# Stick-breaking attention summed by parts, and six of its gates computed as pairs of half-size products

## The chip, the cores and the metric

The kernel runs on one core of one Trainium2 chip, as one program. The metric is the device time of one execution in microseconds (us). Engines are named as in the profile: PE (TensorE matmul), DVE (VectorE), ACT (ScalarE), POOL (GpSimd), SP (SyncE, which here issues nearly all the DMAs from one queue).

## The reference, cut to what matters

One layer with two token mixers over 1024 tokens of width 1024, in float32. The normalized input h is multiplied by one wide matrix; its columns give, for a gated linear attention (GLA, 4 heads), queries, keys, values, gates and a decay code, for stick-breaking attention (8 heads of 128) queries, keys, values and gates, and two merge gates. Each branch is projected, gated and merged; an output projection and a norm follow. What the change touches is stick-breaking:

```
z = q . k / sqrt(d)                       # for every query t and key s
log1m = where(s < t, log_sigmoid(-z), 0)
between = reversed cumsum(log1m) - log1m  # sum over s < j < t
A = where(s < t, exp(log_sigmoid(z) + between), 0)
o = A @ v                                 # then o * silu(s_gate)
```

With beta = sigmoid(z), A[t,s] = beta[t,s] times the product of 1 - beta[t,j] over s < j < t. Let P[t,s] be the product of 1 - beta[t,j] over s <= j < t. Then A[t,s] = P[t,s+1] - P[t,s], and summation by parts turns the sum of A[t,s] v[s] into the sum of P[t,s] (v[s-1] - v[s]) plus one term of v.

## The kernel before, in words

Every float32 operand of a matmul is split into a high part (an ACT copy to float32r, line 165) and a low part (a DVE subtraction, line 166), and each product is three matmuls: high-high, high-low, low-high. Matmuls stream 512 columns where they can.

**Stages in order.** (1) The input is normed and transposed; the four quarters of h (token half by parity of the 128-wide block of D) are held as `a11`, `a12`, `a21`, `a22`. In the same stage a first group of 256 columns of a value projection is computed directly (`first_v`, with the decay code in the same matmuls), and three more groups follow (`v_unit`, `vjobs`): 24 matmuls of 256 columns for each of 8 token blocks. (2) Projections as **pairs** (`pair_job`, lines 235 to 301): two 128-wide column blocks at once in seven half-size products of 12 matmuls each (Strassen's scheme in Winograd's form), so 84 matmuls of 512 columns for 256 output columns and all tokens, against 96 for the direct way. A pair has seven *units*; `Pairs.run(n)` issues n units, with the loads and splits of the next pairs between them. The first 22 units run between the steps of the GLA decays, the units up to number `GLA_AT` between loads, sums and stores of later weights (`tjobs`); in both stretches the order on ACT and DVE is the order of the program. (3) GLA: 32 steps, each with four units of pairs (137 units in all from its start to its last step). (4) **Stick-breaking**, then (5) the merge and the output projection, again as half-size products.

**Stick-breaking** runs over 8 heads of 8 query blocks of 128. For block i, `scores` multiplies queries and keys of the causal prefix (banks `z`, two), takes sigmoid(-z) into `eb` and sigmoid(z) into `be` (ACT, lines 960 and 961), scans `eb` from the right on DVE (line 964, a running product with the diagonal block masked), masks `be` on POOL (line 965) and multiplies the two on DVE (line 968). Two steps later `turn` transposes the result block by block on PE (line 980) and splits it into `near` (diagonal half) and `far` buffers. `values` multiplies these with the split values: 12 matmuls for the first four blocks of a head, 24 for the last four, and multiplies the sum with the gate (line 1004). Queries are loaded two blocks at a time, four steps ahead; keys and values one head ahead.

**Filler.** Between the steps stand *units* of 24 matmuls (`proj_t`): the silu gates of the eight heads in two token halves (16 units) and the first projection of GLA's output (`pa`, 16 units). Two run ahead of the first head; `SB_PLAN` says how many run at each step: three per head (at steps 3 and 6 ahead of the transposes, at step 7 behind them). `line` lists the units in order, with their weight loads and with two loads of GLA's outputs (`o_dma`), which overwrite the quarters of h once the gates no longer read them. Six units are left for the start of stage 5.

**Who sets the order.** Outside the stretches with a manual schedule, the order of each engine's instructions is laid down at build time by a planner that simulates the program and prefers earlier program lines among what is ready; in the trace the matmuls of one filler unit therefore often stand in several places between those of the scores. At run time each engine takes its instructions in that order.

## Time and profile before

| | |
|---|---|
| time, median of 3 runs | 1204.47 us (1201.83 to 1204.98) |
| the profiled execution's own time, and its span | 1205.73 us, 1204.0 us |
| PE busy | 1185.2 us, 98% of the span, 6087 matmuls |
| DVE / ACT / POOL busy | 855.4 (71%) / 555.8 (46%) / 316.7 us (26%) |
| mean granted PE clock | 0.997 |
| moved by DMA | 247.67 MB, mean 206 GB/s |
| first value groups and sums | from the start to about 114 us |
| eight pairs ahead of GLA / GLA with pairs / stick-breaking | 116 to 276, 276 to 711, 720 to 1010 us |

In the profile, a group's row gives line, engine, operation, tiles and shapes, the count, then busy us and mean ns of one, then the engine's idle time just before and what ended it. Matmuls overlap in the pipeline: the mean duration of one is longer than the distance from one start to the next, so PE's work is read from stretches of time, not from durations. `PEld` are weight loads, which run beside the matmuls. A row of stretches gives busy time and number of instructions of each engine between two times.

### The profile page before, as it was taken

The page shows a single profiled execution, that of the slowest core. Times are in us where ns is not written, and L with a number is a line of the kernel's source. Part 1 is how long each engine was busy: PE and PEld are TensorE (multiplying, and loading weights), DVE is VectorE, ACT ScalarE, POOL GpSimd, SP SyncE. Part 2 cuts the span into 40 slices and gives each one's busy share as a digit, 9 for nine tenths or more (in the row PEclk, how much of TensorE's full clock was granted, in tenths as well). Part 3 has the DMA queues.
Part 4 walks back from the last instruction along what each step waited for, and adds up shares of the span by engine and source line. Part 5 has one row for each costly group of instructions (what it writes and reads, how often), then busy time and mean ns, then how long its engine had stood idle before and what let it go on. Part 6 is the DMA issues. An engine that isn't in the chain of part 4 may idle for free.

```text
span 1204.0 us, 17310 instructions
## 1 busy us (share of the span) xinstructions
PE 1185.2 (98%) x6087; PEld 997.8 (83%) x6087; DVE 855.4 (71%) x1341; ACT 555.8 (46%) x1081; POOL 316.7 (26%) x303
## 2 busy tenths in 40 slices
PE   8999999999999999999999999999999999999997
PEld 8999878888888888888888887888878888788886
DVE  5475876896676676776674646777787775578986
ACT  5343763334334444444443425445455553365543
POOL 1486513243322322422323201111021110700001
PEclk9999999999999999999999999999999999999999
DMA  7545349988546646666655267564788547758652
GB/s 282 182 140 154 136 164 337 338 303 265 185 145 197 179 157 210 209 200 204 218 172 166 80 230 259 168 209 159 251 263 304 169 131 242 254 161 282 225 192 105
DMA packets 207090, 247.67 MB, mean 206 GB/s; under 512 B 12662, under 2 KB 141708, under 8 KB 205468
## 3 DMA queue, kind: packets, MB, share of 16 engines
q1 hardware_dynamic: 206428, 245.52, 62.3%
q8 instruction: 48, 0.79, 0.3%
q10 hardware_dynamic: 576, 1.05, 0.2%
q14 instruction: 38, 0.31, 0.1%
HBM read 154.25 MB, written 92.27 MB: 205 GB/s over the span
## 4 chain that ended last, share of the span: by engine, by line
PE 83%; DVE 7%; DMA 3%; ACT 3%; issue 3%; SPq 1%; POOL 0%; DVEq 0%; ACTq 0%
PE pp L270 12%; PE pp L272 12%; PE pp L271 12%; PE pp L223 8%; PE pp L204 4%; PE pp L206 4%; PE pp L205 4%; PE av L1002 2%; PE av L1003 1%; PE z L956 1%; PE av L1001 1%; PE tr L980 1%; PE xb L1368 1%; PE xb L1367 1%; PE z L957 1%
## 5 line engine op out<-in xcount | busy, mean ns | idle before, releaser
L166 DVE TENSOR_TENSOR wl<-tt,wh 128x1024 fp32r<-128x1024 f32 x56 | 70.6, 1261 | 49.6 <-ACT wh L165 49.4
L965 POOL TENSOR_SCALAR_AFFINE_SELECT be<-be 128x128 f32<-128x128 f32 x64 | 38.0, 595 | 236.7 <-ACT be L961 218.3
L309 DVE TENSOR_TENSOR f<-pp,f 128x512 f32<-128x512 f32 x84 | 57.8, 688 | 59.1 <-PE pp L272 55.7
L964 DVE TENSOR_TENSOR_SCAN eb<-eb,m 128x128 f32<-128x128 f32 (+3 forms) x64 | 86.7, 1356 | 9.7 <-ACT eb L960 9.5
L165 ACT ACTIVATE wh<-tt 128x1024 fp32r<-128x1024 f32 x56 | 59.3, 1059 | 67.2 <-PE pp L271 63.8
L244 POOL TENSOR_TENSOR tt<-raw 128x512 f32<-128x512 f32 x28 | 39.5, 1412 | 190.9 <-DVE wl L166 184.2
L165 ACT ACTIVATE wh<-raw 128x1024 fp32r<-128x1024 f32 x47 | 49.7, 1059 | 81.0 <-PE pp L271 39.1
L276 ACT ACTIVATE f<-pp 128x512 f32<-128x512 f32 x84 | 49.7, 592 | 79.9 <-PE pp L272 79.9
L166 DVE TENSOR_TENSOR wl<-raw,wh 128x1024 fp32r<-128x1024 f32 x47 | 70.5, 1501 | 22.4 <-ACT wh L165 21.6
L231 POOL TENSOR_TENSOR r<-r,nhalf 128x1 f32<-128x1 f32 x40 | 24.2, 604 | 193.2 <-DVE r L230 182.7
L960 ACT ACTIVATE eb<-z 128x384 f32<-128x384 f32 (+4 forms) x96 | 48.8, 508 | 43.4 <-issue 22.8
L968 DVE TENSOR_TENSOR be<-be,eb 128x128 f32<-128x128 f32 (+3 forms) x64 | 48.3, 757 | 3.6
L961 ACT ACTIVATE be<-z 128x384 f32<-128x384 f32 (+4 forms) x96 | 49.2, 513 | 0.0
L270 PE MATMUL pp<-ha22h,wh 128*128 128x512 f32 x112 | 44.7, 399 | 0.3 <-DVE f L309 0.2
L270 PE MATMUL pp<-ha11h,wh 128*128 128x512 f32 x112 | 44.5, 397 | 0.0
L270 PE MATMUL pp<-ha12h,wh 128*128 128x512 f32 x112 | 44.5, 397 | 0.0
L270 PE MATMUL pp<-S1h,wh 128*128 128x512 f32 x112 | 44.4, 396 | 0.0
L270 PE MATMUL pp<-S3h,wh 128*128 128x512 f32 x112 | 44.1, 394 | 0.0
L270 PE MATMUL pp<-S2h,wh 128*128 128x512 f32 x112 | 44.0, 392 | 0.0
L270 PE MATMUL pp<-S4h,dh 128*128 128x512 f32 x112 | 43.9, 392 | 0.0
L271 PE MATMUL pp<-ha22l,wh 128*128 128x512 f32 x112 | 43.7, 390 | 0.0
L272 PE MATMUL pp<-ha22h,wl 128*128 128x512 f32 x112 | 43.7, 390 | 0.0
(519 smaller groups left out, 3979.7 us busy)
## 6 DMA issues: line engine op xcount, KB each, us to landing
raw<-in_w_in_dram SPq DMA_DIRECT2D x31, 1024.0 KB, 6.5
d_v<-o SPq DMA_DIRECT2D x32, 256.0 KB, 3.0
d_gv<-o SPq DMA_DIRECT2D x32, 256.0 KB, 4.0
d_t<-t SPq DMA_DIRECT2D x16, 512.0 KB, 4.7
v<-d_gv SPq DMA_DIRECT2D x32, 256.0 KB, 3.5
d_ogl<-o SPq DMA_DIRECT2D x64, 128.0 KB, 2.8
d_q<-o SPq DMA_DIRECT2D x16, 512.0 KB, 5.2
d_k<-o SPq DMA_DIRECT2D x16, 512.0 KB, 3.4
```

Of the source, the lines that this page charges most:

```text
L165: nc.scalar.activation(hi, src, AF.Copy)
L166: eng.tensor_sub(lo, src, hi.bitcast(F32))
L223: nc.tensor.matmul(pt[:, 0:n], *ops[kb][i], start=k == 0, stop=k == 3 * KB - 1)
L270: nc.tensor.matmul(pt, bh[:, j], ah[:, j], start=first and j == 0, stop=False, skip_group_check=True)
L271: nc.tensor.matmul(pt, bh[:, j], al[:, j], start=False, stop=False, skip_group_check=True)
L272: nc.tensor.matmul(pt, bl[:, j], ah[:, j], start=False, stop=j == 3, skip_group_check=True)
L276: nc.scalar.activation(t[nm], t[bank], AF.Copy)
L309: nc.vector.tensor_add(add, bank, add)
L960: nc.scalar.activation(om[:, osl], zt[:, 0:w], AF.Sigmoid, scale=-inv_sqrt)
L961: nc.scalar.activation(be[:, osl], zt[:, 0:w], AF.Sigmoid, scale=inv_sqrt)
L964: nc.vector.tensor_tensor_scan(rest, rest, m1[:, off:T][:, ::-1], 1.0, op0=ALU.mult, op1=ALU.max)
L968: nc.vector.tensor_mul(be[:, off:T], be[:, off:T], om[:, off + 1:T + 1])
```

## The change

- **Summation by parts.** `scores` takes one sigmoid, scans it in place, and that is all: the second sigmoid, POOL's mask and the product go. The transposed matrix is now P, with ones on and above the diagonal of the diagonal block. The values are stored as differences of neighbouring tokens; at a diagonal block the ones add up to v[t-1] minus the block's last value, which is added back when the sum is multiplied with the gate: four operations of 128 columns on DVE where there was one of 512.
- **Differences need the values transposed** (tokens along the row). So the stick-breaking values become pairs (`sv_pair`), which yield that form and are differenced ahead of their transposes; the last value of every block is kept in `vend`. GLA's values take their place as direct projections in stage 1 (`C_GV` for `C_SV`). The number of pairs and of direct groups for the two kinds of values stays as it was.
- **Gates of heads 0 to 5** become three pairs (`sg_pair`) behind the value, query and key pairs. The list of pairs grows from 28 to 31; `GLA_AT` goes from 56 to 77 units, so that GLA still has 137 units and three pairs more lie ahead of it. The loads, sums and stores between units ahead of GLA come every five units, not every three.
- **Filler.** Four gate units and 16 `pa` units are left. Two still run ahead of the first head, six still behind the last; between them even heads have two (steps 3 and 6) and odd heads one (step 6). The first load of GLA's outputs now stands right behind the two opening units.
- **Order.** The values of a head's first half come at step 5 and those of its second half at step 2 of the next head, both ahead of the transposes of that step; they stood at steps 4 and 0, behind them.

```diff
-SB_PLAN = [(0, 0), (0, 0), (0, 0), (1, 0), (0, 0), (0, 0), (1, 0), (0, 1)]
+SB_PLAN = [0, 0, 0, 1, 0, 0, 1, 0]
-GLA_AT = 56
+GLA_AT = 77
...
+    vend = const.tile([P, SB_H, NT], F32, tag="vend", name="vend")
     def store_v(key, i, tb):
-        st = vst.pop((key, tb // 2)) if tb % 2 else None
-        if st is not None:
-            for e in range(2):
-                nc.sync.dma_start(d_v[2 * i + e][:, tb - 1:tb + 1], st[:, :, :, e * P:(e + 1) * P].bitcast(F32))
+        if tb % 2:
+            nc.sync.dma_start(d_gv[i][:, tb - 1:tb + 1], vst.pop((key, tb // 2)).bitcast(F32))
...
-    vjobs = [(i, C_SV + i * DV) for i in range(1, SB_H // 2)]
+    vjobs = [(i, C_GV + i * DV) for i in range(1, GLA_H)]
...
+    def sg_pair(i):
+        return pair_job(w_in, C_SG + i * DV,
+                        lambda J, n, bank, add: silu(total(bank, add), d_sg[2 * i + J][:, half(n)]))
-    def gv_pair(h):
+    def sv_pair(i):
+        held = []
         def evict(J, n, bank, add):
...
+            h = 2 * i + J
+            nc.vector.tensor_copy(vend[:, h, 4 * n:4 * n + 4], add[:, P - 1:HALF:P])
+            held.append((J, n, h, add))
+            if (J, n) != (1, 1):
+                while held:
+                    diff(*held.pop())
+        def diff(J, n, h, add):
+            d = ev.tile([P, HALF], F32, tag="f", name="f")
+            nc.vector.tensor_sub(d[:, 1:HALF], add[:, 0:HALF - 1], add[:, 1:HALF])
+            if n:
+                nc.vector.tensor_sub(d[:, 0:1], vend[:, h, 3:4], add[:, 0:1])
+            else:
+                nc.vector.tensor_scalar(d[:, 0:1], add[:, 0:1], -1.0, None, op0=ALU.mult)
             def turn():
                 pt = ps.tile([P, HALF], F32, tag="tr", name="tr")
                 for b in range(4):
-                    nc.tensor.transpose(pt[:, b * P:(b + 1) * P], add[:, b * P:(b + 1) * P], ident)
+                    nc.tensor.transpose(pt[:, b * P:(b + 1) * P], d[:, b * P:(b + 1) * P], ident)
...
-                  [gv_pair(0)] + gla_qk(0) + [gg_pair(0), gv_pair(1), gg_pair(1)] + gla_qk(1) +
-                  [gv_pair(2), gg_pair(2), gv_pair(3), gg_pair(3)] +
-                  [f for i in range(4) for f in (qk_pair(C_SQ, i, d_q), qk_pair(C_SK, i, d_k))] +
-                  [merge_pair(C_MB, i, d_gb) for i in range(4)] + [merge_pair(C_MA, 3, d_ga)], late)
+                  gla_qk(0) + [gg_pair(0), gg_pair(1)] + gla_qk(1) + [gg_pair(2), gg_pair(3)] +
+                  [f for i in range(4) for f in (qk_pair(C_SQ, i, d_q), sv_pair(i), qk_pair(C_SK, i, d_k))] +
+                  [sg_pair(i) for i in range(3)] + [merge_pair(C_MB, i, d_gb) for i in range(4)] + [merge_pair(C_MA, 3, d_ga)], late)
...
-        at = 3 * k
+        at = 5 * k
...
-        om = ebuf[i % 2]
-        be = bets.pop("first", None)
-        if be is None:
-            be = sb.tile([P, T], F32, tag="be", name="be", bufs=3)
-        bets[h, i] = be
+        om = bets[h, i] = sb.tile([P, T], F32, tag="be", name="be", bufs=4)
...
-            nc.scalar.activation(om[:, osl], zt[:, 0:w], AF.Sigmoid, scale=-inv_sqrt)
-            nc.scalar.activation(be[:, osl], zt[:, 0:w], AF.Sigmoid, scale=inv_sqrt)
+            nc.scalar.activation(om[:, off + pc * w:off + (pc + 1) * w], zt[:, 0:w], AF.Sigmoid, scale=-inv_sqrt)
         rest = om[:, off:T][:, ::-1]
         nc.vector.tensor_tensor_scan(rest, rest, m1[:, off:T][:, ::-1], 1.0, op0=ALU.mult, op1=ALU.max)
-        nc.gpsimd.affine_select(be[:, T - P:T], be[:, T - P:T], pattern=[[-1, P]],
-                                compare_op=ALU.is_gt, fill=0.0, base=0,
-                                channel_multiplier=1)
-        nc.vector.tensor_mul(be[:, off:T], be[:, off:T], om[:, off + 1:T + 1])
...
-        nc.vector.tensor_mul(gate, pav, gate)
+        for q in range(4):
+            cs = slice(q * P, (q + 1) * P)
+            nc.vector.scalar_tensor_tensor(gate[:, cs], pav[:, cs], vend[:, h, 4 * g + q:4 * g + q + 1], gate[:, cs],
+                                           op0=ALU.add, op1=ALU.mult)
...
-    line = [gate_load(0), gate_load(1)]
-    for h in range(5):
-        line += [gate_load(h + 2), gate(h, 0), gate(h, 1)]
-    line += [gate(5, 0), gate_load(7), gate(6, 0), gate(7, 0), o_dma(0), gate(5, 1), pa_load(0), gate(6, 1), pa_load(1),
-             gate(7, 1), o_dma(1), pa_load(2), pa(0, 0), pa(1, 0), pa(2, 0)]
+    line = [gate_load(6), gate_load(7), gate(6, 0), gate(7, 0), o_dma(0), gate(6, 1), pa_load(0), gate(7, 1), o_dma(1),
+            pa_load(1), pa_load(2), pa(0, 0), pa(1, 0), pa(2, 0)]
...
-        st.run(SB_PLAN[i][0])
+        st.run(SB_PLAN[i] if i == 6 or h % 2 == 0 else 0)
+        if i == 2 and h:
+            values(h - 1, 1)
+        elif i == 5:
+            values(h, 0)
         turn(h, i)
-        st.run(SB_PLAN[i][1])
-        if i % 4 == 0 and s:
-            values(*((h, 0) if i else (h - 1, 1)))
```

More of the change, by code (lines that the diff above doesn't have):

```diff
@@ L379, in load_vr @@
             rows = w_in[4 * i * P:(4 * i + 4) * P, :]
-            nc.sync.dma_start(raw[:, :, 0:DV], rows[:, C_SV:C_SV + DV].rearrange("(k p) c -> p k c", p=P))
+            nc.sync.dma_start(raw[:, :, 0:DV], rows[:, C_GV:C_GV + DV].rearrange("(k p) c -> p k c", p=P))
             nc.sync.dma_start(raw[:, :, DV:VR], rows[:, C_GR:C_GR + RANK].rearrange("(k p) c -> p k c", p=P))
@@ L604, in turn @@
                 for b in range(4):
-                    nc.tensor.transpose(pt[:, b * P:(b + 1) * P], add[:, b * P:(b + 1) * P], ident)
+                    nc.tensor.transpose(pt[:, b * P:(b + 1) * P], d[:, b * P:(b + 1) * P], ident)
                 o = stage()
                 split(pt, o[:, 0], o[:, 1])
-                for i in range(2):
-                    nc.sync.dma_start(d_gv[h][:, 4 * n:4 * n + 4, i, J * P:(J + 1) * P],
-                                      o[:, i].bitcast(F32).rearrange("p (b c) -> p b c", c=P))
+                for e in range(2):
+                    nc.sync.dma_start(d_v[h][:, 4 * n:4 * n + 4, e],
+                                      o[:, e].bitcast(F32).rearrange("p (b c) -> p b c", c=P))
             late.append(turn)
-        return pair_job(w_in, C_GV + h * DV, evict)
+        return pair_job(w_in, C_SV + i * DV, evict)
     def gla_qk(i):
@@ L918, in hybrid_layer @@
     bets = {}
-    ebuf = [sb.tile([P, T + 16], F32, tag=f"eb{i}", name=f"eb{i}", bufs=1) for i in range(2)]
     m1 = sb.tile([P, T], F32, tag="m1", name="m1", bufs=1)
@@ L924, in hybrid_layer @@
                             base=0, channel_multiplier=1)
-    for e in ebuf:
-        nc.gpsimd.memset(e[:, T:T + 1], 1.0)
-    bets["first"] = sb.tile([P, T], F32, tag="be", name="be", bufs=3)
     wraw = raw_tile()
```

1 line of the change is left out of this document (removed).

## The prediction

> **What bounds the kernel now.** I read the page's busy times first, then stretches of the span, then who TensorE waited for. From the page:
>
> ```profile
> span 1204.0 us, 17310 instructions
> PE 1185.2 (98%) x6087; PEld 997.8 (83%) x6087; DVE 855.4 (71%) x1341; ACT 555.8 (46%) x1081; POOL 316.7 (26%) x303
> PEclk9999999999999999999999999999999999999999
> ```
>
> PE is busy 98% of the span at full granted clock, so a saving must shorten PE's own stream or its waits. The stretches (columns: length, then busy us and instruction count of PE, PEld, DVE, ACT, POOL, then clock, DMA share, GB/s):
>
> ```profile
> core 0: us, PE busy (x) PEld busy (x) DVE busy (x) ACT busy (x) POOL busy (x), PEclk, DMA share, GB/s
> 115.62:275.62 160.00, 159.49 (x715) 130.15 (x713) 126.25 (x145) 77.32 (x100) 57.55 (x40) 1.00 0.74 254
> 275.62:711.44 435.82, 435.82 (x2167) 358.77 (x2166) 291.12 (x601) 192.29 (x410) 130.30 (x118) 1.00 0.59 182
> 711.40:719.70 8.30, 8.30 (x39) 6.91 (x38) 3.55 (x6) 1.80 (x3) 1.62 (x6) 1.00 1.02 394
> 719.70:1009.70 290.00, 284.51 (x1490) 240.40 (x1490) 216.50 (x279) 147.18 (x333) 38.05 (x64) 1.00 0.64 211
> 216.50:235.54 19.04, 19.04 (x86) 15.77 (x84) 16.04 (x17) 5.50 (x7) 7.23 (x4) 1.00 1.01 352
> 785.81:791.27 5.46, 5.46 (x26) 4.46 (x25) 5.46 (x7) 1.71 (x6) 1.46 (x1) 1.00 0.81 261
> 765.33:972.48 207.15, 204.50 (x1081) 173.48 (x1079) 158.87 (x206) 105.66 (x244) 29.23 (x47) 1.00 0.65 216
> ```
>
> The first row is the eight pairs ahead of GLA, the second GLA with pairs between its steps, the third the last units of pairs, the fourth stick-breaking (two filler units, then eight heads). The fifth is exactly one pair, from its first product to the next pair's: 19.04 us for 84 matmuls, 0.227 us each. The sixth is exactly one gate unit of 24 matmuls: 5.46 us, 0.2275 us each (the counts take in a neighbour or two at the edges). The last is six whole heads, from one head's first transpose to the same place six later: 34.5 us a head. PE never waits in GLA and only 5.5 us in stick-breaking:
>
> ```profile
> PE av L1002 <- DVE atl L166: 3.1, 3, 1.5
> PE z L956 <- ACT be L961: 1.6, 4, 0.7
> PE pp L980 <- DVE be L968: 0.4, 1, 0.4
> PE tr L980 <- DVE be L968: 0.3, 1, 0.3
> ```
>
> So today the sigmoids, scans and splits of stick-breaking are hidden behind three filler units per head, and whatever they take off VectorE and ScalarE gives almost nothing by itself.
>
> **Part 1, the matmuls.** Twelve gate units (heads 0 to 5, two halves) leave stick-breaking: 12 x 5.46 = 65.5 us. Three pairs come ahead of it: 3 x 19.04 = 57.1 us. Net -8.4 us of pure PE stream. The values' and GLA-values' projections only change places: four groups of 256 columns stay direct, four stay pairs with 64 transposes in all, so PE's share of that is zero.
>
> **Part 2, what the moved pairs drag along, costed at nothing.** GLA keeps its number of pair units (137); the three extra pairs lie ahead of it. POOL gets 3 x 4 sums more there:
>
> ```profile
> L244 POOL TENSOR_TENSOR tt<-raw 128x512 f32<-128x512 f32 x28 | 39.5, 1412 | 190.9 <-DVE wl L166 184.2
> L965 POOL TENSOR_SCALAR_AFFINE_SELECT be<-be 128x128 f32<-128x128 f32 x64 | 38.0, 595 | 236.7 <-ACT be L961 218.3
> ```
>
> 12 x 1.41 = 17 us on an engine that is busy 57.6 of 160 us. On SP's queue six 512 KB weight loads become three of 1024 KB, twelve gate stores move ahead, the direct values' store goes in one transfer of 512 KB where it took two of 256 KB, and the loads and stores of the transposed weights come every five units, not three: 160 us at a DMA share of 0.74 become 217, with 1 MB of weights added per pair. Each stick-breaking value pair now gives VectorE, beside what a pair did, four differences, four copies of block ends and four one-column fixes. The nearest difference of two SBUF tiles, 128x512, costs 0.82 us, the copies and fixes are nearest to a 128x8 copy:
>
> ```profile
> L166 DVE TENSOR_TENSOR o<-f,o 128x512 fp32r<-128x512 f32 x24 | 19.6, 816 | 4.7 <-ACT o L165 4.1
> L857 DVE SCALAR_TENSOR_TENSOR g<-tr,vcol,g 128x128 f32<-128x128 f32 x40 | 12.1, 343 | 10.1 <-PE tr L854 10.1
> L770 DVE COPY fac<-ebl 128x8 f32<-128x8 f32 x1 | 0.2, 165 | 0.0
> ```
>
> 4 x (0.82 + 2 x 0.165) = 4.6 us a pair, 18.4 us in all, on a VectorE that is busy 291 of 436 us there (67%; 71% after). PE covers it. Without that cover it costs between 0 and 18.4 us; I take 0, as PE's idle time in that row is zero.
>
> **Part 3, what stick-breaking loses.** VectorE and ScalarE in the six heads (groups with busy us and mean ns):
>
> ```profile
> L964 DVE TENSOR_TENSOR_SCAN eb<-eb,m 128x512 f32<-128x512 f32 (+7 forms) x47 | 64.1, 1364 | 8.4 <-ACT eb L960 8.4
> L968 DVE TENSOR_TENSOR be<-be,eb 128x512 f32<-128x512 f32 (+7 forms) x47 | 35.8, 762 | 2.6
> L166 DVE TENSOR_TENSOR atl<-tr,ath 128x128 fp32r<-128x128 f32 (+3 forms) x48 | 22.6, 474 | 2.0 <-ACT ath L165 2.0
> L166 DVE TENSOR_TENSOR afl<-pp,afh 128x512 fp32r<-128x512 f32 x24 | 16.4, 684 | 0.0
> L166 DVE TENSOR_TENSOR wl<-raw,wh 128x1024 fp32r<-128x1024 f32 x9 | 11.0, 1225 | 11.3 <-ACT wh L165 11.1
> L570 DVE TENSOR_TENSOR o<-pp,o 128x512 f32<-128x512 f32 x12 | 8.3, 688 | 6.3 <-ACT o L569 6.3
> L1004 DVE TENSOR_TENSOR f<-av,f 128x512 f32<-128x512 f32 x12 | 8.2, 686 | 13.3 <-PE av L1003 13.3
> L1044 DVE TENSOR_TENSOR o<-pp,o 128x512 f32<-128x512 f32 x7 | 4.8, 688 | 5.7 <-PE pp L206 5.6
> L961 ACT ACTIVATE be<-z 128x512 f32<-128x512 f32 (+4 forms) x71 | 36.6, 516 | 0.0
> ```
>
> The product with the second sigmoid (35.8/6 = 6.0 us of VectorE a head), that sigmoid (36.6/6 = 6.1 us of ScalarE) and POOL's mask go. A score bank is then free after one sigmoid, so the wait of L956 goes, and the values of a second half come at step 2 of the next head, not at step 0, so two of the three waits of L1002 go (the third, 1.5 us, is at the stage's start). Between 0 and 5.4 us come back; I take 2.
>
> **Part 4, whether half the filler still covers the rest.** A head is 34.5 us with three units, so 34.5 - 16.4 = 18.1 without. After the change a head with two units takes 29.0 us, one with a single unit 23.6. VectorE a head: scans 10.7, splits 3.8 + 2.7, the values' eviction 8 x 0.343 = 2.7 (four pieces where there was one; L857 is the nearest form), and (11.0 + 8.3 + 4.8)/18 = 1.34 a unit: 22.6 us of 29.0 (78%) and 21.3 of 23.6 (90%); together 43.9 of 52.6, 83%, against 171.2/6 = 28.5 of 34.5, also 83%, now. The balance is as before on average and tight in the odd heads.
>
> Where it is tightest can be placed. Scores run two steps ahead of their transposes. At a head's start the steps are short and hold no unit: between the scores of block 1 and its transposes PE has only the last transposes of the old head, the scores of blocks 2 and 3 and one transpose. The same boundary now, VectorE's order in time (start, length), then PE's:
>
> ```profile
> 861.03 0.55 DVE L166 TENSOR_TENSOR atl<-tr,ath 128x384 fp32r<-128x384 f32 x1
> 861.50 0.68 DVE L166 TENSOR_TENSOR afl<-pp,afh 128x512 fp32r<-128x512 f32 x1
> 862.10 0.68 DVE L964 TENSOR_TENSOR_SCAN eb<-eb,m 128x256 f32<-128x256 f32 x1
> 862.69 0.67 DVE L166 TENSOR_TENSOR atl<-tr,ath 128x512 fp32r<-128x512 f32 x1
> ...
> 860.28 0.36 PE L956 MATMUL z<-k,q 128*128 128x256 f32 x1
> 860.72 0.60 PE L980 MATMUL tr<-ident,be 128*128 128x128 f32 x4
> 861.51 0.48 PE L204 MATMUL pp<-ha21h,wh 128*128 128x512 f32 x1
> ```
>
> Block 1's scan ends at 862.78. After the change PE finishes the old head's transposes at 861.51 as here, then scores of blocks 2 and 3 (3 x 0.17 and 3 x 0.2275) and one transpose of 0.1: block 1's transposes are due at 862.8. That is no cover at all, but just no stall. If the two splits of the old head's last transposes (0.67 + 0.68) go ahead of the scan, it is 1.4 us late, and the values of the old head's second half wait on those splits otherwise. So 0 to 1.4 us at each of the seven boundaries. Into an even head the planner can pull that head's first unit forward; into an odd head (four times) there is none near. PE takes its instructions in the order written, so whatever follows block 1 waits with it: the scores of block 4 and the long values behind them. I take 0.8 x 4 = +3.2 us, the row's 0 and the bound weighed about equally; the bounds are 0 and 9.8.
>
> **Part 5, a transfer that jumps the queue.** With only four gate units left, the load of the GLA outputs (four of 1024 KB, which wait for the last first-half gate) is issued right after the two opening units, where it used to come after eleven more units, in the fourth head. On SP's queue it now stands ahead of the third query tile of head 0 (256 KB), and of head 1's keys and values. Median landings:
>
> ```profile
> oa11l<-d_ogl SPq DMA_DIRECT2D x1, 1024.0 KB, 5.4
> oa12l<-d_ogl SPq DMA_DIRECT2D x1, 1024.0 KB, 11.0
> q<-d_q SPq DMA_DIRECT2D x32, 256.0 KB, 3.8
> ```
>
> The queries would land about 11.0 instead of 3.8 us after their place in the queue: 7.2 us late at worst, 0 at best, because a whole gate unit (5.46 us) is ready to stand in. I take +1.2. [...]
>
> **The sum.** -8.4 - 2.0 + 3.2 + 1.2 = -6.0 us. The profiled execution took 1205.7 us (span 1204.0 and 1.7 around it), so 1199.7; the median of the runs, 1204.5, lies 1.2 lower, so 1198.5.
>
> **Rivals.** (a) Everything tightens: the waits of Part 3 all go and no boundary stalls. 1204.5 - 8.4 - 5.4 = 1190.7. For it: the scan that ends just in time. Against: 90% of VectorE in the odd heads.
>
> (b) The gain is given back at the start of stick-breaking: the queue of Part 5 costs its full 7.2 us. 1204.5 - 8.4 - 2.0 + 3.2 + 7.2 = 1204.5, no change. For it: the DMA engines are full (1.02) just ahead of the stage. Against: the planner moved gate matmuls between late scores in every head so far. [...]
>
> (c) Slower: VectorE becomes the bound in the odd heads. In the six heads its rows fill 83% of the time, and nothing shows that it can do more as a link in the chain from sigmoid through scan and transposes to split. If that is its ceiling, it needs 21.3/0.83 = 25.7 us for an odd head and 27.2 for an even one, so odd heads lose 2.1 us each, 8.4 in all, which eats the gain; with the boundary bound of 9.8 us on top it is 1204.5 - 8.4 - 2.0 + 8.4 + 9.8 = 1212.3. It decides from 2.1 us per odd head. Against it: consecutive VectorE instructions overlap (861.03 + 0.55 ends after 861.50 began), and its idle time now is mostly waiting for PE.
>
> **Chances.** Forecast 0.50, (a) 0.17, (b) 0.18, (c) 0.15. A difference under 0.3%, 3.6 us, can't be told from no change. Faster than 1200.9: most of the forecast (0.42), (a), a little of (b): 0.62. Within: 0.23. Slower than 1208.1: (c) and a tail of (b): 0.15. The forecast's own range is 1194 to 1203; to leave out no more than 2 in 10 the range reaches from 1189 into (c), to 1209.
>
> **What would show it.** Right: stick-breaking (first filler unit to last value matmul) shrinks from 290.0 to about 290 - 65.5 + 2 = 227 us, while the stretch ahead grows by 57; even heads of about 29 and odd of about 23.6 us; L956 no longer waits for ScalarE; the few waits of PE name the scan or a split at block 1 of odd heads. Part 5 shows as a gap before block 4's scores of head 0. Wrong: pairs dearer than 19.1 us in GLA with PE waiting for VectorE's differences (Part 2); odd heads over 25.7 us (c); or both head lengths below 28 and 23 (a).

## The result, and the profile after

The changed kernel took 1220.05 us (median of four runs, 1218.35 to 1226.86) beside 1204.72 us for the kernel before in the same session: a ratio of 1.0148 with a 95% interval of 1.0129 to 1.0167. The forecast of 1198.5 us and its range of 1189 to 1209 were wrong: the change made the kernel slower, by some 15 us. The profiled execution took 1226.86 us, with a span of 1225.1 us. It is the longest of the four, 6.8 us above the median, so the waits and the clock read from it below are somewhat larger than in a usual execution, and its accounts close against its own 21.1 us, not against 15.3.

From the page of the changed kernel:

```profile
span 1225.1 us, 17001 instructions
PE 1186.7 (97%) x6051; PEld 997.6 (81%) x6051; DVE 838.6 (68%) x1388; ACT 537.4 (44%) x1000; POOL 296.0 (24%) x249
PEclk9999999999999999999999999989999999999999
```

There are 36 matmuls fewer than before, as intended, yet PE's busy time rose by 1.5 us, and one slice of the clock row shows an 8 where the kernel before had only 9s. Both point at slower matmuls somewhere. The stretches of the changed kernel (length, then busy us and count of PE, PEld, DVE, ACT, POOL, then clock, DMA share, GB/s) say where:

```profile
114.10:327.20 213.10, 212.76 (x939) 175.01 (x937) 156.27 (x182) 96.63 (x126) 73.38 (x54) 1.00 0.68 233
327.20:779.64 452.44, 448.64 (x2229) 367.78 (x2228) 301.17 (x652) 198.81 (x418) 133.15 (x120) 1.00 0.55 177
...
779.64:1035.00 255.36, 233.00 (x1213) 197.12 (x1212) 162.70 (x242) 102.90 (x217) 0.00 (x0) 0.95 0.66 220
1035.00:1225.10 190.10, 182.85 (x807) 150.78 (x805) 149.73 (x212) 91.15 (x150) 28.50 (x24) 1.00 0.61 210
```

The first row is the eleven pairs ahead of GLA, the second GLA with the last units of pairs, the third stick-breaking, the fourth the end. Against the boundaries shown of before (719.70 and 1009.70): stick-breaking starts 59.9 us later (57.1 were forecast), is 34.6 us shorter (63 were forecast), and the end is 4.2 us shorter. Together +21.1 us, which is the difference of the two spans. The boundary at the end is not quite the same place: the stage has 1213 matmuls, where 1490 less twelve units of 24 would be 1202, and the end has ten fewer than before, so some 2.5 us of the end's filler now stand ahead of it. The loss lies in stick-breaking: 22.4 us of it are idle for PE, and the mean clock is 0.95. Whom PE waited for, from GLA to the end of stick-breaking (us in total, times, longest):

```profile
PE z L970 <- DMA q<-d_q: 15.4, 5, 4.3
PE z L970 <- ACT be L973: 2.8, 2, 1.7
PE tr L626 <- DVE o L165: 2.1, 2, 1.1
...
PE tr L626 <- DVE f L621: 0.9, 2, 0.6
PE tr L874 <- DVE o L165: 0.8, 1, 0.8
```

15.4 us go to five waits for a load of queries, at the scores of block 4 in heads 0, 1, 3, 4 and 6 (807.76, 840.30, 890.50, 917.50 and 977.80): a wait that is not among the rows of the kernel before. **Why that load is late** begins in `load_q`. It has two buffers: query tiles 0 and 2 of a head (blocks 0, 1 and 4, 5) share one, tiles 1 and 3 the other. Tile 2 can be issued only when the scores of block 1 have read tile 0, and that is done at step 7 of the head before; the scores of block 4 need tile 2 at step 2. Before, PE's order between the two held a filler unit (5.5 us, the one behind the transposes of step 7) and the values of the old head (4.6 us). One such place in the kernel before, SP's issue and the first use (start, length):

```profile
826.48 0.52 SPq L903 DMA_DIRECT2D q<-d_q  x1
...
839.35 0.39 PE L956 MATMUL z<-k,q 128*128 128x320 f32 x1
```

12.87 us lie between issue and use, for a load with a median of 3.8 us. Two such places in the changed kernel, heads 3 and 4: SP's issues for head 3, then PE (the square brackets hold idle time and what ended it; the row at 884.50 is the last score of block 1):

```profile
879.97 0.32 SPq L1016 DMA_DIRECT2D d_osb<-f  x1
885.82 0.32 SPq L999 DMA_DIRECT2D f<-d_sg  x1
...
886.71 0.52 SPq L923 DMA_DIRECT2D q<-d_q  x1
...
884.50 0.28 PE L972 MATMUL z<-k,q 128*128 128x256 f32 x1
...
887.01 0.44 PE L988 MATMUL tr<-ident,be 128*128 128x128 f32 x2
...
890.50 0.38 PE L970 MATMUL z<-k,q 128*128 128x320 f32 x1 [2.15 <-DMA q<-d_q]
890.72 0.31 PE L971 MATMUL z<-k,q 128*128 128x320 f32 x1
890.87 0.31 PE L972 MATMUL z<-k,q 128*128 128x320 f32 x1
...
917.50 0.61 PE L970 MATMUL z<-k,q 128*128 128x320 f32 x1 [3.66 <-DMA q<-d_q]
917.90 0.47 PE L971 MATMUL z<-k,q 128*128 128x320 f32 x1
918.17 0.47 PE L972 MATMUL z<-k,q 128*128 128x320 f32 x1
```

The filler unit behind step 7 is gone, and the values of the old head now stand behind the scores of block 4 in the program. From the issue at 886.71 PE had transposes and three value matmuls to do; it then sat until the load had landed.

**The buffer is not the whole of it: SP's queue makes the issue later still.** In head 3 block 1 is scored at 884.78, and the tile could have been issued then. But it went out at 886.71, behind a gate load (L999) that stands ahead of it in SP's order, and that one went out only at 885.82, when the store at 879.97 had landed (5.8 us). SP's waits of this kind in stick-breaking, in all:

```profile
SPq L999 <- DMA d_osb<-f: 33.0, 8, 5.5
```

In the kernel before they are 4.1 us, in two places. (Why the gate load waits for that store, with five buffers for its tile, the trace does not tell.) From the end of block 1's scores to PE being ready for block 4 there are now 3.6, 3.7 and 3.6 us in heads 3, 4 and 6. The issue came 1.9, 1.6 and 1.5 us into that time, where the kernel before had it 0.03 to 0.05 us behind block 1 in five of eight heads. In heads 2 and 5, where it came 0.1 and 0.5 us behind, PE does not wait for queries.

Heads 0 and 1 are another case. Their buffer is free at 791.40 and 823.71, and 12.1 and 13.5 us pass until PE is ready for block 4, far more than a landing of 3.8 us. But SP issues the tile 3.7 and 8.2 us late, behind loads of GLA's outputs (and, in head 1, behind a value load that waits 4.7 us for its buffer), and it lands 12.58 and 8.37 us after its issue. In head 0:

```profile
794.45 0.59 SPq L1081 DMA_DIRECT2D oa12l<-d_ogl  x1
795.13 2.18 SPq L923 DMA_DIRECT2D q<-d_q  x1
```

So 7.4 of the 15.4 us are the queue's alone, and 8.0 us are a thin cover together with an SP that is held up. Before, the filler covered both: in heads 4 and 5 of that kernel the tile was issued 10.6 and 11.7 us late, behind such loads (a value load alone waited 7.2 and 7.3 us), and PE did not wait, because 16 us of work lay between.

**Four of the five gaps cost twice.** Behind the gap at 917.50 matmuls of 320 columns start 0.27 us apart, behind the one at 890.50 0.15 us. In the changed kernel these are the stretches at half clock:

```profile
807.20:814.00 6.80, 6.24 (x20) 5.59 (x21) 3.43 (x4) 2.40 (x5) 0.00 (x0) 0.50 0.51 170
841.30:844.70 3.40, 3.31 (x11) 2.88 (x11) 1.81 (x2) 1.76 (x5) 0.00 (x0) 0.50 0.25 93
916.40:923.20 6.80, 5.70 (x16) 4.87 (x17) 1.53 (x2) 1.60 (x3) 0.00 (x0) 0.50 0.36 121
950.50:953.90 3.40, 3.38 (x11) 3.00 (x12) 3.40 (x6) 1.15 (x3) 0.00 (x0) 0.51 0.71 222
977.90:981.30 3.40, 3.40 (x11) 3.02 (x12) 1.10 (x1) 1.48 (x3) 0.00 (x0) 0.51 0.30 101
```

PE was busy for 22 us of these at half speed, which loses some 11 us, as an estimate. With the waits that makes 26 us, of the 28.4 by which the stage is longer than the forecast 227. Not every spell is the query's: the one at 950.50 follows waits of 1.74 us for a sigmoid and 0.46 us for a split.

### The profile page after: what moved, and what is told of

Read it like the earlier page. It is cut to its first block, busy times and chain, and to the rows that moved or that the text cites. A ratio compares the mean times of both kernels' runs of the same rounds, so it can differ in the third digit from the quotient of the medians.

```text
span 1225.1 us, 17001 instructions
## 1 busy us (share of the span) xinstructions
PE 1186.7 (97%) x6051; PEld 997.6 (81%) x6051; DVE 838.6 (68%) x1388; ACT 537.4 (44%) x1000; POOL 296.0 (24%) x249
## 3 DMA queue, kind: packets, MB, share of 16 engines
q1 hardware_dynamic: 188716, 245.52, 59.9%
## 4 chain that ended last, share of the span: by engine, by line
PE 84%; DVE 5%; DMA 4%; ACT 3%; issue 2%; POOL 1%; SPq 0%; ACTq 0%; DVEq 0%
PE pp L269 14%; PE pp L270 14%; PE pp L271 14%; PE pp L222 8%; DMA q<-d_q 3%; PE pp L203 3%; PE pp L204 3%; PE pp L205 3%; PE z L970 2%; PE z L972 1%; PE z L971 1%; PE av L1010 1%; PE av L1011 1%; PE av L1009 1%; PE xb L1377 1%
## 5 line engine op out<-in xcount | busy, mean ns | idle before, releaser
L165 DVE TENSOR_TENSOR wl<-tt,wh 128x1024 fp32r<-128x1024 f32 x62 | 77.6, 1252 | 57.5 <-ACT wh L164 57.2
L308 DVE TENSOR_TENSOR f<-pp,f 128x512 f32<-128x512 f32 x93 | 64.0, 688 | 74.9 <-PE pp L271 71.7
L243 POOL TENSOR_TENSOR tt<-raw 128x512 f32<-128x512 f32 x31 | 45.6, 1471 | 248.9 <-DVE wl L165 241.4
L976 DVE TENSOR_TENSOR_SCAN be<-be,m 128x128 f32<-128x128 f32 (+3 forms) x64 | 86.2, 1349 | 25.2 <-ACT be L973 25.2
L164 ACT ACTIVATE wh<-tt 128x1024 fp32r<-128x1024 f32 x62 | 65.6, 1058 | 68.6 <-PE pp L270 68.1
L165 DVE TENSOR_TENSOR wl<-raw,wh 128x1024 fp32r<-128x1024 f32 x44 | 65.5, 1490 | 11.5 <-ACT wh L164 10.8
L1160 POOL TENSOR_TENSOR N<-A,A 128x512 f32<-128x512 f32 x4 | 6.6, 1646 | 272.4 <-DMA A<-d_osb 272.4
L970 PE MATMUL z<-k,q 128*128 128x384 f32 (+4 forms) x96 | 40.4, 421 | 18.2 <-DMA q<-d_q 15.4
L164 ACT ACTIVATE ath<-tr 128x128 fp32r<-128x128 f32 (+1 forms) x64 | 28.0, 439 | 58.2 <-PE tr L988 58.2
L271 PE MATMUL pp<-ha11h,wl 128*128 128x512 f32 x124 | 48.6, 392 | 0.0
L271 PE MATMUL pp<-ha12h,wl 128*128 128x512 f32 x124 | 48.4, 390 | 0.0
```

Source lines behind the costliest of these rows:

```text
L164: nc.scalar.activation(hi, src, AF.Copy)
L165: eng.tensor_sub(lo, src, hi.bitcast(F32))
L243: nc.gpsimd.tensor_sub(t1, b[:, 0, 1], b[:, 0, 0])
L271: nc.tensor.matmul(pt, bl[:, j], ah[:, j], start=False, stop=j == 3, skip_group_check=True)
L308: nc.vector.tensor_add(add, bank, add)
L970: nc.tensor.matmul(zt[:, 0:n], q[:, 0], k[:, 0, ksl], start=True, stop=False)
```

## The experiments

The theory after the result (Theory Q in the expectations): the query tile's buffer, freed late and no longer covered, is what makes the change slow, through the waits and the clock behind them. It left out SP's order, which the rows above add. The rivals were the new order of values and transposes by itself, the early load of GLA's outputs that fills SP's queue (Part 5), the engines VectorE and ScalarE in heads with little filler (rival c), and the new arithmetic. The ratios are to the kernel before, run on the same chip.

### Four query buffers a head

```diff
 def load_q(h, m):
-    t = sw.tile([P, 4, P], F32R, tag="d" + "hl"[m % 2], name="q", bufs=1)
+    if m < 2:
+        t = sw.tile([P, 4, P], F32R, tag="d" + "hl"[m], name="q", bufs=1)
+    else:
+        t = sb.tile([P, 4, P], F32R, tag=f"q{m}", name="q", bufs=1)
```

> The changed kernel with four query tiles per head in place of two that alternate, so that the third tile of a head no longer waits until block 1 of that head has been scored. Theory Q (the load of the third query tile can only start after block 1's scores, and its 3.7 us no longer fit into the 2.3 us of PE work left ahead of block 4): the 15.4 us in which scores wait for queries fall below 2, the stretches at half clock go, and the time falls from 1220 to about 1197 us (1193 to 1201). Rival V (VectorE and ScalarE are the bound in the short heads and the query wait only stands in front of it): other waits take its place, 1212 or more. Rival O (the early 4 MB load of GLA's outputs delays the queries): the waits in heads 0 and 1 (4.3 and 3.1 us) stay, about 1208.

1212.48 us, ratio 1.0063 (1.0047 to 1.0080): 7.6 us, about half of the loss, came back, where Theory Q had expected all of it. The time is one that Rival V had named, but the wait is not V's: four of the five query waits are gone, and the one left, in head 1, is longer than any. The waits of PE, then a whole head from the values of head 0 (821.00) to those of head 1, the stretch at half clock inside it, and two more heads:

```profile
PE z L973 <- DMA q<-d_q: 10.8, 1, 10.8
PE tr L991 <- DVE be L979: 2.9, 4, 1.4
```

```profile
821.00:860.91 39.91, 25.85 (x133) 21.46 (x132) 22.61 (x33) 14.07 (x28) 0.00 (x0) 0.87 0.89 296
832.50:842.70 10.20, 3.59 (x12) 3.35 (x12) 3.56 (x3) 3.48 (x5) 0.00 (x0) 0.50 1.00 336
860.91:889.94 29.03, 29.00 (x162) 25.32 (x162) 20.62 (x33) 13.67 (x31) 0.00 (x0) 1.00 0.80 249
889.94:912.60 22.66, 22.66 (x133) 19.76 (x132) 18.59 (x29) 12.04 (x26) 0.00 (x0) 1.00 0.63 206
```

The heads behind it have the forecast lengths, 29.0 and 22.7 us against 29.0 and 23.6, with PE busy throughout. What is left is SP's queue in head 1. Its issues, start and length:

```profile
820.53 0.52 SPq L1084 DMA_DIRECT2D oa22h<-d_ogl  x1
825.63 0.33 SPq L916 DMA_DIRECT2D v<-d_v  x1
826.02 0.43 SPq L1084 DMA_DIRECT2D oa22l<-d_ogl  x1
826.50 5.49 SPq L180 DMA_DIRECT2D raw<-in_w_pa_dram  x2
832.03 3.42 SPq L926 DMA_DIRECT2D q<-d_q  x1
```

The second load of GLA's outputs (four of 1024 KB), a value load and two weight loads stand ahead of the query tile. SP is held up, first 4.5 us at the value load, which waits for value matmuls to free its buffer, then in the issues themselves, with the DMA engines' share at 0.93 to 1.08, and the query is issued only at 832.03, although its buffer had been free for long. In heads 3, 4 and 6 the tile is now issued 20.8, 15.2 and 15.1 us ahead of its use, and in head 0 at 788.65, ahead of the first load of GLA's outputs. So buffers of their own take the query out of both kinds of delay in those four heads. In head 1 the queue, a cause already there, is all that is left.

### The old head's values ahead of the scores of block 4

```diff
+        if i == 2 and h:
+            values(h - 1, 1)
         if s + 2 < len(steps):
             scores(*steps[s + 2])
         st.run(SB_PLAN[i] if i == 6 or h % 2 == 0 else 0)
-        if i == 2 and h:
-            values(h - 1, 1)
-        elif i == 5:
+        if i == 5:
             values(h, 0)
```

> The changed kernel with one exchange: at step 2 the values of the old head's second half (4.6 us of PE) stand ahead of the scores of block 4, not behind them. Theory Q: the load of 3.7 us has 6.9 us of PE ahead of its use in heads 1 to 7, only head 0 still waits (4.3 us): about 1202 us (1198 to 1207). Against that the values may now wait up to 0.9 us a head for the splits of the last transposes. Rival V: no gain beyond 5 us, 1215 or more. Rival O: heads 0 and 1 keep their waits, about 1208.

1215.59 us, ratio 1.0094 (1.0075 to 1.0113), where Theory Q had expected 1202. The query waits fall from 15.4 to 9.8 us (three, longest 3.9), four spells of 3.4 us at half clock remain. The waits of heads 3 and 6 are gone; those of heads 0 and 1, which the queue makes, stay, and so does head 4's (3.3 us, with a landing of 6.4 us). With the values back in place as cover a part of the loss goes, with the same two buffers.

### The first load of GLA's outputs one unit later

```diff
-line = [..., gate(7, 0), o_dma(0), gate(6, 1), pa_load(0), gate(7, 1), o_dma(1),
+line = [..., gate(7, 0), gate(6, 1), pa_load(0), o_dma(0), gate(7, 1), o_dma(1),
```

> The changed kernel with the first load of GLA's outputs one unit later (behind the third gate unit and its weight load), so that it no longer stands ahead of head 0's third query tile. Theory Q: only head 0's wait (4.3 us and some half clock) can go, about 1214 us (1211 to 1219). Rival O: heads 0 and 1 lose their waits and what follows, about 1207 or less.

1225.97 us, ratio 1.0176 (1.0151 to 1.0202), no better than the change itself. Head 0's wait is gone, as expected, so the place of the first load did cause it; but the two loads come closer together, head 1's wait grows from 3.1 to 7.4 us, and the query waits are again 15.4 us in all. Moving the load moved its cost to the next head.

### The kernel before with the new order

All 24 filler units and the old arithmetic; only the places of filler, values and transposes are the new ones.

```diff
-SB_PLAN = [(0, 0), (0, 0), (0, 0), (1, 0), (0, 0), (0, 0), (1, 0), (0, 1)]
+SB_PLAN = [0, 0, 0, 2, 0, 0, 1, 0]
...
-        st.run(SB_PLAN[i][0])
+        st.run(SB_PLAN[i])
+        if i == 2 and h:
+            values(h - 1, 1)
+        elif i == 5:
+            values(h, 0)
         turn(h, i)
-        st.run(SB_PLAN[i][1])
-        if i % 4 == 0 and s:
-            values(*((h, 0) if i else (h - 1, 1)))
```

> The kernel before, whole in its arithmetic and its 24 filler units, in the new order: the unit behind step 7 moves to step 3, values at steps 5 and 2 ahead of the transposes. Theory Q: the cover of the third query tile falls from about 13 us to 2.3 us here too, with three units per head: query waits of 2 us or more in most heads and stretches at half clock, 1204.7 + 15 to 25 us = 1220 to 1230. Rival V: with all filler in place nothing waits, 1204 to 1210.

1205.54 us, ratio 1.0009 (0.9999 to 1.0019), a miss for Theory Q, which had counted on waits from the new order. PE's largest waits:

```profile
PE z L956 <- ACT be L961: 3.2, 3, 2.6
PE z L956 <- DMA q<-d_q: 2.6, 4, 1.1
```

Waits for queries appear in four places, 1.1 us at most, and the clock does not fall. The cover did shrink as the theory said: in head 3 block 1 is scored at 828.75 and PE is ready for block 4 only 2.7 us later, less than the 3.6 us of the changed kernel. But SP issues the tile at once here (828.77), it lands in 3.7 us, and PE waits 1.1. SP's waits for output stores are 11.7 us, against 33.0 in the changed kernel. So the new order alone makes the cover thin and does little harm; most of the harm comes when SP, with the thinned filler, is late as well. No run changes SP's order by itself.

### Four buffers, and the second load of GLA's outputs in two halves

```diff
 (with the edit of load_q)
-gate(7, 1), o_dma(1), pa_load(1), pa_load(2), pa(0, 0), pa(1, 0), pa(2, 0)]
+gate(7, 1), pa_load(1), pa(0, 0), o_dma(1, (0,)), pa_load(2), pa(1, 0), o_dma(1, (1,)), pa(2, 0)]
```

> The changed kernel with four query tiles per head and the second load of GLA's outputs cut in two halves of 2 MB, each one filler unit later than the one before (behind the first and second unit of the first projection), in place of four of 1024 KB in one place in head 0. Theory Q+O (two causes: the third query tile's late issue in every head, and the second 4 MB load that stands ahead of head 1's queries on the same queue): the one wait of 10.8 us that the four tiles left, and its 10.2 us at half clock (about 5 us of work), go: 1212.5 - 16 = 1197 us (1194 to 1200), faster than before. Rival V (a bound on VectorE in short heads): other waits in its place, 1205 or more.

1200.83 us (11 runs), ratio 0.9972 (0.9960 to 0.9983): the loss is gone, and some 3.4 of the forecast 6.0 us of gain are there. The stage as a whole, then heads 1, 3 and 5 (from step 2 of each to step 2 of the next):

```profile
779.81:1008.70 228.89, 222.82 (x1213) 189.99 (x1212) 162.51 (x242) 102.69 (x217) 0.00 (x0) 0.99 0.74 244
...
820.46:847.42 26.96, 24.39 (x132) 20.90 (x133) 21.47 (x33) 12.73 (x28) 0.00 (x0) 0.95 0.87 298
...
876.49:900.65 24.16, 23.70 (x135) 20.29 (x135) 19.30 (x30) 13.45 (x31) 0.00 (x0) 1.00 0.83 278
...
929.92:953.08 23.16, 23.12 (x137) 20.25 (x135) 19.91 (x32) 11.44 (x27) 0.00 (x0) 1.00 0.71 224
```

228.9 us with the same 1213 matmuls for which the changed kernel needs 255.4, and 227 were forecast: of the difference of 26.5 us, 16.3 are idle time and 10.2 are PE's busy time for the same matmuls, which is what the waits and the clock came to above. What PE still waits for, from GLA to the end of stick-breaking:

```profile
PE z L973 <- ACT be L976: 3.3, 4, 2.4
PE tr L626 <- DVE o L165: 2.0, 2, 1.0
...
PE z L973 <- DMA q<-d_q: 0.5, 1, 0.5
```

### The same halves with the two old buffers

```diff
-gate(7, 1), o_dma(1), pa_load(1), pa_load(2), pa(0, 0), pa(1, 0), pa(2, 0)]
+gate(7, 1), pa_load(1), pa(0, 0), o_dma(1, (0,)), pa_load(2), pa(1, 0), o_dma(1, (1,)), pa(2, 0)]
```

> The changed kernel with its two alternating query tiles, and only the second load of GLA's outputs cut and spread as in the run with four tiles. Theory Q+O: head 1's query wait (3.1 us and 3.4 us at half clock) goes, those of heads 0, 2, 3 and 5 (12.3 us and 17 us at half clock) stay: 1215 us (1212 to 1219). If O alone were the cause: under 1205.

1220.28 us, ratio 1.0133 (1.0116 to 1.0150), as the change itself and a little above the expected range; the query waits are 12.1 us (five, longest 3.6) and four spells run at half clock (23.8 us in all). They stand in heads 0, 1, 2, 4 and 6 (heads counted from 0; the heads that the expectation calls 2, 3 and 5 are 3, 4 and 6 in the rows above). Head 1 still waits 2.2 us: its tile is issued 0.04 us behind block 1 now, but lands only 6.5 us later, and its cover has shrunk to 4.4 us. So spreading the load by itself gains nothing with two buffers; the queue's part can be taken out only together with the buffer's.

### Also one late transposition a unit

The wait of L626 for L165 in the rows of the four-buffer version is in GLA: transposes of a moved value pair wait for a split to give a bank free. Here at most one late transposition is issued per unit, where all that were due came at once.

```diff
 (Pairs.run, with the four buffers and the two halves)
-            due = self.late[:]
-            self.late.clear()
+            due = self.late[:1]
+            del self.late[:1]
```

> The kernel of the run before with one more edit: where a pair of stick-breaking values gives two blocks to transpose in one unit, the second is transposed one unit later. Theory T (in the GLA stage the two transposes take both banks and the next GLA transposes wait; 5 us dearer than the pairs' own matmuls): 3 to 5 us faster than the run before, about 1193. Rival: the stage is dearer for another reason (planner order, VectorE's share), no change beyond 1 us.

1199.36 us, ratio 0.9963 (0.9950 to 0.9977). The wait of L626 for that split is gone and stick-breaking starts at 777.9 instead of 779.8 us; the gain is some 1.5 to 2 us where 3 to 5 had been expected, and the two intervals overlap. It has the lowest median of all versions, 0.2 us under the next. The largest wait left, 2.5 us once, is a score behind a busy bank; ScalarE's order explains it:

```profile
841.93 1.06 ACT L164 ACTIVATE wh<-raw 128x1024 fp32r<-128x1024 f32 x1 [2.32 <-DMA raw<-in_w_pa_dram]
842.89 0.36 ACT L976 ACTIVATE be<-z 128x256 f32<-128x256 f32 x1
```

The sigmoid that frees the bank stands behind the split of a weight load which has not landed: again a load that landed late (7.1 us).

### All of these, with the values ahead of the scores

```diff
 (with the four buffers, the halves and the single late transposition)
+        if i == 2 and h:
+            values(h - 1, 1)
         if s + 2 < len(steps):
             scores(*steps[s + 2])
...
-gate(7, 1), pa_load(1), pa(0, 0), o_dma(1, (0,)), pa_load(2), pa(1, 0), o_dma(1, (1,)), pa(2, 0)]
+gate(7, 1), pa_load(1), pa(0, 0), pa_load(2), o_dma(1, (0,)), pa(1, 0), o_dma(1, (1,)), pa(2, 0)]
```

> The kernel with four query tiles, the spread second load and one late transpose per unit, with two more edits: at step 2 the old head's values stand ahead of the scores of block 4, and the third weight load of the first projection stands ahead of the first half of the spread load, not behind it. In the run without them one wait of 2.5 us and 3.4 us at half clock remained in head 2, where ScalarE stood at the split of a weight tile that landed late. Theory Q+O: that wait goes, 3 to 4 us faster: 1196 us (1193 to 1199). Rival: the values ahead of the scores wait for the splits of the last transposes instead, no gain or 1 to 3 us lost.

1199.56 us, ratio 0.9960 (0.9947 to 0.9974), the same as without, as the rival had it. There is no query wait left, but the waits on score banks are 5.9 us (four, longest 2.7). The two edits together gain nothing more once the queries have their own buffers; which of them does what, this run does not show.

### Summation by parts alone

Sixteen gate units and three a head, the old order and plan, 28 pairs with eight ahead; scores, values and value pairs are the new ones.

```diff
 (the changed kernel)
-GLA_AT = 77
+GLA_AT = 56
-SB_PLAN = [0, 0, 0, 1, 0, 0, 1, 0]
+SB_PLAN = [(0, 0), (0, 0), (0, 0), (1, 0), (0, 0), (0, 0), (1, 0), (0, 1)]
-[sg_pair(i) for i in range(3)] + [merge_pair(C_MB, i, d_gb) for i in range(4)]
+[merge_pair(C_MB, i, d_gb) for i in range(4)]
```

> Summation by parts alone: the stick-breaking values as pairs with differences and one sigmoid per score, but all sixteen gates as filler units and three units per head where they stood before (28 pairs, 8 of them ahead of GLA, values at steps 0 and 4 behind the transposes). Theory Q: with the old filler no query waits: before's time, plus about 5 us for the pairs' transposes in GLA, minus 2 to 5 us of waits in stick-breaking: 1202 to 1208. Rival V or a cost of the new arithmetic itself (longer waits on the scan, four evictions): 1212 or more.

1205.16 us (10 runs), ratio 1.0009 (0.9999 to 1.0018). Stick-breaking, then PE's waits in it:

```profile
725.60:1010.40 284.80, 282.86 (x1489) 240.14 (x1488) 177.96 (x260) 113.39 (x237) 0.00 (x0) 1.00 0.66 215
```

```profile
PE z L970 <- ACT be L973: 0.9, 1, 0.9
PE z L970 <- DMA q<-d_q: 0.6, 2, 0.4
```

The stage is 5.2 us shorter than before and the waits there are nearly gone, as Part 3 had it at its upper bound; but it starts at 725.6 instead of 719.7 us. The moved pairs give back ahead of it what the sigmoids save in it: 3.8 us in which transposes wait (L626 and L874, as in the changed kernel) and 2.3 us in which a pair waits for its sums. ScalarE's busy time in the stage falls by 23% (147.18 to 113.39 us), and all that comes of it while filler covers it is a part of those 5.2 us.

### The gates as pairs alone

The old arithmetic (two sigmoids, mask, product), with the new filler, order and three pairs.

```diff
 (the kernel before)
-SB_PLAN = [(0, 0), (0, 0), (0, 0), (1, 0), (0, 0), (0, 0), (1, 0), (0, 1)]
+SB_PLAN = [0, 0, 0, 1, 0, 0, 1, 0]
-GLA_AT = 56
+GLA_AT = 77
+[sg_pair(i) for i in range(3)] +
```

> The other part alone: the kernel before with its two sigmoids, mask and product, but the gates of heads 0 to 5 as three pairs, three filler units per two heads and the new order. Theory Q: the query waits of the changed kernel come here too, and VectorE has 6.0 us a head more, 25.9 us less one unit's share in heads where PE has 23.6: 1225 us or more (1222 to 1240). Rival V2 (the new arithmetic with its four evictions and in-place scan makes the short heads wait): 1196 to 1204, since PE's stream is the same 8.4 us shorter.

1227.51 us, ratio 1.0194 (1.0175 to 1.0214). Its waits:

```profile
PE z L961 <- DMA q<-d_q: 14.6, 7, 3.6
PE tr L985 <- DVE be L973: 5.5, 10, 1.6
```

The query waits are those of the changed kernel (14.6 against 15.4 us), so the new arithmetic does not cause them; SP waits 32.2 us for output stores here too. The new arithmetic does help where filler is thin: without it transposes wait 5.5 us for the product on VectorE, a wait the changed kernel does not have.

## Why the prediction was wrong

**Part 1** held. Eleven pairs take 213.1 us, and stick-breaking starts 59.9 us later for 57.1 forecast; PE's busy time is 8.5 us shorter in the version with four buffers and halves (1176.7 against 1185.2 us), for 8.4 forecast. Its parts: stick-breaking 60.1 us later, a stage of 228.9 in place of 290.0, an end shorter by 4.2, together -5.2 us of span, for -6.0 forecast. The two have not quite the same terms: the end's 4.2 us were not in the sum. 2.7 us of them are the ten matmuls that now stand ahead of the boundary; the other 1.5 us are idle time of PE, and their cause stays open.

**Part 2** costed the moved work at nothing, with PE's idle time in GLA as the reason. The row 327.20:779.64 now has 3.8 us of it, and the three waits of L626 and L874 (2.1, 0.9 and 0.8 us) are exactly this. They are not for the differences that I priced alone, but mostly (2.9 us) for the splits behind them, which hold a transposition bank. With summation by parts alone the stage started 5.9 us later, in the changed kernel 2.8 us later than Part 1's 57.1. The term that was put at nothing is 3 to 6 us, inside its bounds of 0 and 18.4.

**Part 3** held in kind: the waits of the second sigmoid went. No separate gain can be told from it.

**Part 4 failed**, and it is the step that the forecast hung on. It counted what the removed filler covers as the work of VectorE and ScalarE, and placed the tightest point at block 1's scan, in four odd heads, at 3.2 us. The changed kernel has no wait for that scan among its rows; the version with four query buffers has 2.9 us (L991) in four places, all around head 1 (816 to 846), and the version with halves 1.2 us. What the filler also covered was a transfer, and the queue that issues it: 3.7 to 4.2 us from issue to landing, once per head, and 1.5 to 8.2 us by which SP issues late in the five heads that wait. That cost 15.4 us of waiting, and most of the 11 us of clock. The prediction quoted the boundary of two heads in PE's and VectorE's order and never put SP's issue of the query tile beside it. Its note that the scores of block 4 and the long values behind them wait together came true, for another reason: in head 3 PE sat 2.15 us ahead of the scores at 890.50, and the values behind them start at 891.45.

**Part 5** saw that a transfer would jump the queue, and sized it for head 0 alone: at most 7.2 us, taken as 1.2. In the chain of waits of the changed kernel the query load of head 0 took 12.58 us and PE waited 4.27; with half of the 6.2 us of work at half clock behind it that is about 7.4 us, the whole of the bound. With filler halved, however, the second load of GLA's outputs also moved, into head 1, and that was left out altogether; it cost 10.8 us of waiting in the first experiment, and made head 1 39.9 us long where the version with halves needs 27.0. In that experiment the loads landed in the order of their issue: those issued at 820.01, 820.53, 825.63 and 832.03 landed at 827.4, 829.9, 832.7 and 839.0. But the larger part of head 1's delay came ahead of that, in SP's own issuing (832.03).

**Rival (b)** had the mechanism, a query load behind the queue, but in one head, and it ended at no change. The rival that happened, a load in every head whose late buffer and late issue the filler had covered, was not among them. **Rival (c)** did not happen: odd heads with PE fed take 23 to 24 us, below its 25.7, although VectorE is busy 80 to 86% of them.

**The clock** has no term in the sum; by the estimate above it cost about 11 us over five spells. No length of a gap sorts the falls. The clock fell within the gaps of 4.27 and 3.66 us (at 807.2 and 916.4; they ended at 807.76 and 917.50). But it also fell at 977.9, right after 2.15 us that ended at 977.80, while 2.15 us that ended at 890.50 had no spell behind them. The fall can also come late: the gap of 3.14 us ended at 840.30, and the clock fell at 841.3.

The idle time in short stretches does sort them. The spells last 3.4 or 6.8 us and start at 807.2, 841.3, 916.4, 950.5 and 977.9, which is 10, 22, 10 and 8 times 3.41 us apart (170.7 us from the first to the last, 50 times 3.41). Laid out in stretches of 3.41 us from the first spell, the stick-breaking stage of the changed kernel has PE idle for 3.41, 2.40, 2.62, 1.57 and 2.15 us in the stretches just ahead of the five spells, and for 1.39 us at most in any other stretch at full clock. The 2.15 us ahead of 977.80 lie in one stretch; those ahead of 890.50 lie in two, 0.8 and 1.4 us. So in this run PE's idle time within a stretch, in one gap or several, sorts the falls, and the length of a gap does not. Whether it holds beyond this run is not shown.

## What to carry to other kernels

Before thinning filler, list every load whose buffer comes free only inside the thinned stretch, and hold its issue-to-use distance in the new order against its landing time; the engines' busy shares (PE 98%, DVE 71% of the span before) did not show it here. Then read what stands ahead of it in the issuing engine's queue and what that waits for: a buffer that is free in time does not help a load that is not issued (head 1 of the first experiment, 832.03). When work is taken out of a stage, everything tied to a count of units (loads of the next stage, here 8 MB) moves to another place in the stage, and each such place has to be costed. A fix of one late load can uncover the next one in the same queue: buffers alone gave back half of the loss, the spread alone nothing, both together all of it.

## What the runs showed of the hardware that was not expected

- Waits of 2 us amid short matmuls already led to spells of 3.4 us at half clock (977.9 us after one of 2.15; 950.5 us after 1.74 and 0.46), and one of the same length did not (890.50 us). The idle time in stretches of 3.41 us, laid out from the first spell, sorts them in the changed kernel: 1.57 to 3.41 us ahead of the five spells, 1.39 us at most elsewhere at full clock.
- SP's issues were not of constant length. A 256 KB query load is issued in 0.52 us at the median of 32 in the changed kernel, and in 2.18 us at 795.13; in the first experiment, with up to 2.5 MB issued ahead of it and not yet landed, and the DMA engines' share at 1.08, the issue took 3.42 us, and that of two weight loads ahead of it 5.49.
- A late store held up the loads behind it in SP's order: in three heads of the changed kernel a gate load went out within 0.05 us of the landing of a store (885.82, 910.85 and 972.63; the stores took 5.8, 5.0 and 4.8 us), and the query load behind it 0.9 us later (886.71, 911.73 and 973.55).
